# Attention queries turned two heads at a time, with the sum of squares on GpSimd

## The chip, the cores and the metric

The kernel runs on one core of one Trainium2 chip. A core has TensorE (PE; its weight loads are shown apart as PEld), VectorE (DVE), ScalarE (ACT), GpSimd (POOL) and SyncE (SP, which issues DMAs). Each engine takes its own instructions in order, and semaphores hold an instruction until what it needs is done. The metric is the device time of one execution in microseconds; less is better. Before the change it is 1444.52 us, the median of 3 runs (1444.01 to 1444.83).

## The reference, cut to what matters

One encoder layer is computed for two sequences of 512 tokens, with a model width of 1024. The input is normalized and projected to queries, keys, values, the input of a state-space branch and two gates. The state-space branch and a windowed attention branch are gated, added and projected, and a squared-ReLU MLP follows. All is float32. The part that the change touches is the norm of the queries in front of the attention:

```python
def rms_norm(x, g):
    xf = x.astype(jnp.float32)
    y = xf * lax.rsqrt(jnp.mean(xf * xf, axis=-1, keepdims=True) + EPS)
    return (y * g.astype(jnp.float32)).astype(x.dtype)

    q = rms_norm(q.reshape(bsz, seq_len, N_HEADS, HEAD_DIM), q_gain)   # 16 heads of 64
    k = rms_norm(k.reshape(bsz, seq_len, N_KV_HEADS, HEAD_DIM), k_gain)  # 4 heads of 64
    ...
    # a block of 128 queries sees the key blocks before it, at it and behind it
    s = jnp.einsum('nqkgd,njkd->nkgqj', qb, kw).astype(jnp.float32) * scale + bias
    s = jnp.where(mask[:, None, None], s, NEG_INF)
    p = jax.nn.softmax(jnp.concatenate([s, sink_col], axis=-1), axis=-1)[..., :-1]
    o = jnp.einsum('nkgqj,njkd->nqkgd', p.astype(vs.dtype), vw)
```

## The kernel before

The kernel works in stages: the load and norm of the input with the first projections, the state-space branch with the other projections between its parts, attention, the gated merge, the output projection, and the MLP. Products of float32 matrices are made in three passes from a high and a low part of each operand (a value rounded to the format fp32r, and what is left of it).

**Attention** goes over 8 steps (`steps`): 4 groups of heads `j` (one key head with its G = 4 query heads) times 2 sequences `sq`. A step has 4 units, one for each block `qb` of 128 queries; so there are 32 units. The first and the last block of a sequence see 2 key blocks, the others 3. The order of the work is written out by hand for PE, ACT, DVE and POOL; SP's DMAs follow their data. Three things run interleaved in a unit:

- `cur`, the unit itself. Per head `h`: `scores(h)` (PE, two passes, with the high and the low part of the keys), `largest(h)` (DVE, adds the bias and takes the maximum, L974), `exp(h)` (ACT, L980). Two PSUM buffers (`sps`) serve the four heads.
- `prev`, the unit before. Per key block `i`: `turn(i)` (PE, 4 transposes of the probabilities, L986), `high(i)` (ACT, L990), `low(i)` (DVE, L995), `value(i, part)` (PE, L1002). At the end `lower_part` (ACT, L1006), and in the next unit `add` (DVE, L1012).
- `new`, the tile of 128 queries of the *next* step: `project(n)` issues the next n of its 24 matmuls (L919). They fill PE between the other work. At the unit's end `square` (ACT, L925) squares the projected queries into `sq`.

In the unit after that, the tile is called `rows`. `power` sums the squares of each head (DVE, L929), adds EPS (POOL, L931) and takes the power -1/2 (POOL, L932). `norm` scales the queries (DVE, L936). `turn` makes one transpose for each of the 4 heads (PE, L941); each puts the 64 values of a head on partitions 0 to 63, in its quarter of one PSUM tile. `high` (ACT, L946) writes the high part, times the gain, to partitions 0 to 63 of the query tile `qa`, and `low` (DVE, L949) the low part to partitions 64 to 127. The key tiles hold the same 64 key values on both halves of the partitions, so that one pass of the scores multiplies the keys with high plus low part.

The order around the change, in a unit: `power` comes first; on POOL the copy of the sink into `p` (L962) stands ahead of it, and behind it stand, as far as the unit has them, pieces of the merge's operands (`y_lows`, L1066, in steps 6 and 7), the copy of the next step's keys (`key_copies`, L888, in the first unit of a step) and the low part of a weight piece (`lower`, L874 or L786). `norm` stands on DVE behind `low(0)` of `prev` and ahead of `largest(2)`. Behind `largest(3)` PE has `rows.turn`, `prev.turn(2)` (the other way round in steps 6 and 7), `key_turn` of the next keys (L901, first unit of a step), `div.turn` (second unit), four matmuls of the projection, then `rows.high`, `rows.low`, `prev.high(2)`, `prev.low(2)`, and `value(1, 0)`, `exp(3)`, four matmuls, `value(1, 1)`, four matmuls, `value(2, 0)`, `value(2, 1)`, `new.square`. From step 1 on, DVE multiplies the output of the step before with the gate at the end of the third unit (`gated`, L1047) and with the softmax's factors at the end of the fourth (`multiply`, L1051, steps 1 to 6).

Ahead of the first step a loop over t = 0 to 3 projects the first step's 4 query tiles, with `square`, `power` and `norm` at once and `turn`, `high` and `low` one tile later; the last tile is turned in the first unit. In the last step there is no next step; there `project` issues the first matmuls of the merge's product (L125).

Of the kernel before, what the change touches and what calls it, by code (L numbers as in the profile page):

```python
# [64 lines left out]
def hybrid_layer(ctx, tc, x, x_t, w_kv, rel, onehot, w_qkv, w_ug, vectors, lam, coefs, w_glu, w_out, ln2,  # L65
# [772 lines left out]
    with tc.tile_pool(name="att", bufs=2, reuse_waits="tile") as ap, tc.tile_pool(name="attc", bufs=1, reuse_waits="tile") as ac:  # L838
# [67 lines left out]
        class Tile:  # L906
# [20 lines left out]
            def power(self):  # L927
                ms = small.tile([P, G], F32, tag="ms", name="ms")
                V.reduce_sum(ms, self.sq, axis=AX.X)  # L929
                self.rq = small.tile([P, G], F32, tag="rq", name="rq")  # L930
                GP.tensor_scalar_add(ms, ms, EPS)  # L931
                GP.tensor_tensor(self.rq, ms, neg_half[:, 0:G], op=ALU.pow)  # L932
# [5 lines left out]
            def turn(self):  # L938
                self.pt = self.pt or acc()
                for h in range(G):  # L940
                    PE.transpose(self.pt[0:64, h * P:(h + 1) * P], self.qn[:, h], ident)  # L941

            def high(self):
                self.ptv = self.pt[0:64].rearrange("p (h t) -> p h t", h=G)
                self.dst = queries[self.key][:, :, self.t * P:(self.t + 1) * P]
                S.activation(self.dst[0:64], self.ptv, AF.Copy, scale=gain_q[0:64])  # L946

            def low(self):
                V.scalar_tensor_tensor(self.dst[64:128], self.ptv, gain_q[0:64], self.dst[0:64].bitcast(F32),  # L949
                                       op0=ALU.mult, op1=ALU.subtract)  # L950
# [152 lines left out]
        with tc.manual_schedule(engines={ET.PE, ET.DVE, ET.Activation, ET.Pool}):  # L1103
# [14 lines left out]
            for t in range(4):  # L1118
# [5 lines left out]
                new.power()  # L1124
# [36 lines left out]
        with tc.manual_schedule(engines={ET.PE, ET.Activation, ET.DVE, ET.Pool}):  # L1161
            for i, (j, sq) in enumerate(steps):
# [4 lines left out]
                for qb in range(NB):  # L1167
# [36 lines left out]
                    if rows and not rows.qn:  # L1204
                        rows.norm()
# [17 lines left out]
                    if n3:  # L1223
                        prev.low(1)
                        prev.value(0, 1)
                    cur.largest(3)
                    if n3 > 2 and i > 5:
                        prev.turn(2)
                    if rows:
                        rows.turn()  # L1230
                    if n3 > 2 and i < 6:
# [6 lines left out]
                    if n3 > 2 and i > 5:  # L1238
                        prev.high(2)
                        prev.low(2)  # L1240
                    if rows:
                        rows.high()
                        rows.low()
                    if n3 > 2 and i < 6:
                        prev.high(2)
                        prev.low(2)
                    if n3:
                        prev.value(1, 0)
                    cur.exp(3)
                    project(4)  # L1250
                    if n3:
# [606 lines left out]
```

## Time and profile before

| | us |
|---|---|
| median of 3 runs | 1444.52 |
| profiled execution | 1445.04 |
| its span, first to last instruction | 1443.3 |
| PE busy | 1435.6 |
| DVE busy | 1094.9 |
| ACT busy | 762.3 |
| POOL busy | 244.1 |
| attention stage, about 436 to 655: length | 219.0 |
| PE / DVE / ACT / POOL busy in it | 217.9 / 195.1 / 183.9 / 92.1 |

The clock granted to TensorE was full throughout. Matmuls overlap, so the duration of one (272 ns for a 128x128 transpose) is longer than the time for which it holds PE; that is read from the starts of instructions that follow one another. In the rows of the timeline the first number is the start in microseconds from the span's start, the second the duration of the merged run of instructions, then follow engine, line, operation, output and inputs, shape and count, and in brackets the idle time before it with what ended it. In the rows of groups the count is followed by the busy time in microseconds, the mean duration of one in nanoseconds, and the idle time ahead of them.

### The profile page before, as it was taken

To read this page: it belongs to the slowest core of one execution; us is meant where nothing else is said; L and a number is where in the kernel's file an instruction comes from. 1 tells how busy PE (TensorE), PEld (TensorE's weight loads), DVE (VectorE), ACT (ScalarE), POOL (GpSimd) and SP (SyncE) were. 2 spreads that over 40 slices of the span, in tenths; PEclk is the share of its full clock that TensorE was granted. 3 is DMA by queue.
4 is the path that set the end of the run, shared out by engine and by line. 5 is a ranking of instruction groups with operands and counts; after the bars stand their busy time and mean duration, and the time that the engine had idled before them with its cause. 6 is when DMAs were issued, how large, how long until landed. Compare 5 with 4: busy or idle time off the path is not lost.

```text
span 1443.3 us, 22044 instructions
## 1 busy us (share of the span) xinstructions
PE 1435.6 (99%) x7997; PEld 1228.0 (85%) x7997; DVE 1094.9 (76%) x1978; ACT 762.3 (53%) x1359; POOL 244.1 (17%) x396
## 2 busy tenths in 40 slices
PE   9999999999999999999999999999999999999998
PEld 8888888889999999988888888888888888888887
DVE  7999959995458999988976588777776597575644
ACT  7678861224448887894444255455454443333332
POOL 3144443004244432263100000000000000000000
PEclk9999999999999999999999999999999999999999
DMA  7356549529651533345552344444442983464341
GB/s 297 97 170 189 168 147 327 206 91 314 227 180 59 162 107 100 119 140 189 194 190 91 129 136 173 161 160 155 151 143 96 363 319 102 146 201 145 121 131 59
DMA packets 102204, 240.23 MB, mean 166 GB/s; under 512 B 12330, under 2 KB 25130, under 8 KB 102096
## 3 DMA queue, kind: packets, MB, share of 16 engines
q1 hardware_dynamic: 62304, 139.94, 29.9%
q0 software_dynamic: 16320, 48.28, 10.2%
q10 hardware_dynamic: 23472, 50.61, 9.5%
q8 instruction: 63, 1.03, 0.3%
q14 instruction: 45, 0.37, 0.1%
HBM read 169.02 MB, written 81.82 MB: 174 GB/s over the span
## 4 chain that ended last, share of the span: by engine, by line
PE 84%; DVE 8%; issue 4%; DMA 2%; ACT 1%; POOL 1%; DVEq 0%; SPq 0%; ACTq 0%; POOLq 0%
PE bank L118 14%; PE bank L120 14%; PE bank L119 14%; PE acc L187 9%; PE acc L125 6%; PE acc L919 5%; PE po L1002 2%; PE sps L970 2%; PE sps L641 2%; PE tps L986 2%; PE sps L753 2%; PE acc L120 2%; PE acc L119 2%; PE acc L118 2%; DVE t L716 2%
## 5 line engine op out<-in xcount | busy, mean ns | idle before, releaser
L187 PE MATMUL acc<-act,c_hi 128*128 128x512 f32 x768 | 243.7, 395 | 0.0
L119 PE MATMUL bank<-b_lo,a_hi 128*128 128x512 f32 (+1 forms) x449 | 174.4, 389 | 0.0
L120 PE MATMUL bank<-b_hi,a_lo 128*128 128x512 f32 (+1 forms) x449 | 174.4, 389 | 0.0
L118 PE MATMUL bank<-b_hi,a_hi 128*128 128x512 f32 (+1 forms) x449 | 174.4, 389 | 0.0
L187 PEld LDWEIGHTS acc<-act,c_hi 128*128 128x128 f32 x768 | 142.3, 188 | 27.8 <-ACT act L316 0.9
L1714 ACT CAST a_hi<-d_a 128x1024 fp32r<-128x1024 f32 x56 | 59.1, 1055 | 177.4 <-PE bank L119 173.2
L187 PE MATMUL acc<-act,c_lo 128*128 128x512 f32 x384 | 151.3, 394 | 0.0
L1715 DVE TENSOR_TENSOR a_lo<-d_a,a_hi 128x1024 fp32r<-128x1024 f32 x56 | 68.5, 1223 | 98.5 <-ACT a_hi L1714 98.5
L118 PE MATMUL bank<-act,act 128*128 128x512 f32 x368 | 143.2, 389 | 0.0
L119 PE MATMUL bank<-act,act 128*128 128x512 f32 x368 | 143.2, 389 | 0.0
L120 PE MATMUL bank<-act,act 128*128 128x512 f32 x368 | 143.2, 389 | 0.0
L919 PE MATMUL acc<-w_hi,act 128*128 128x256 f32 x512 | 114.0, 291 | 0.1
L119 PEld LDWEIGHTS bank<-b_lo,a_hi 128*128 128x128 f32 x449 | 84.3, 188 | 17.5
L120 PEld LDWEIGHTS bank<-b_hi,a_lo 128*128 128x128 f32 x449 | 84.3, 188 | 17.5
L118 PEld LDWEIGHTS bank<-b_hi,a_hi 128*128 128x128 f32 x449 | 84.3, 188 | 17.3
L919 PEld LDWEIGHTS acc<-w_hi,act 128*128 128x128 f32 x512 | 87.0, 189 | 4.0 <-PE sps L970 0.3
L187 PEld LDWEIGHTS acc<-act,c_lo 128*128 128x128 f32 x384 | 72.2, 188 | 14.7 <-DVE c_lo L178 0.8
L125 PE MATMUL acc<-act,gc_hi 128*128 128x512 f32 x256 | 81.2, 394 | 0.3 <-POOL act L1066 0.3
L118 PEld LDWEIGHTS bank<-act,act 128*128 128x128 f32 x368 | 69.1, 188 | 14.4
L120 PEld LDWEIGHTS bank<-act,act 128*128 128x128 f32 x368 | 69.1, 188 | 14.3
L119 PEld LDWEIGHTS bank<-act,act 128*128 128x128 f32 x368 | 69.1, 188 | 14.2
L980 ACT ACTIVATE p<-p,nmx 128x257 f32<-128x257 f32 (+1 forms) x128 | 72.0, 563 | 16.5 <-DVE nmx L974 15.5
(365 smaller groups left out, 3424.4 us busy)
## 6 DMA issues: line engine op xcount, KB each, us to landing
d_a<-a_scr SPq DMA_DIRECT2D x56, 512.0 KB, 3.6
raws<-in_w_up_dram SPq DMA_DIRECT2D x32, 512.0 KB, 4.0
a_scr<-t ACTq DMA_DIRECT2D x64, 256.0 KB, 3.0
k<-in_w_down_dram SPq DMA_DIRECT2D x32, 512.0 KB, 5.6
c_raw<-in_w_ug_dram SPq DMA_DIRECT2D x48, 256.0 KB, 4.1
ct_scr<-ctab POOLq DMA_DIRECT2D x16, 512.0 KB, 4.8
ctab_in<-ct_scr POOLq DMA_DIRECT2D x16, 512.0 KB, 6.4
a_scr<-a ACTq DMA_DIRECT2D x32, 256.0 KB, 2.0
```

What stands on the lines that cost most here:

```text
L118: PE.matmul(ps, a[0], b[0], start=first, stop=False)
L119: PE.matmul(ps, a[0], b[1], start=False, stop=False)
L120: PE.matmul(ps, a[1], b[0], start=False, stop=last)
L125: PE.matmul(ps, w[wi][:, k, :], rows[yi], start=k + p == 0, stop=k == KT - 1 and p == 2)
L187: PE.matmul(ps, w[wi][:, k, :], hT[s][hi][:, k, :], start=n == 0, stop=n == 3 * KT - 1)
L641: PE.matmul(ps[:, i * P:(i + 1) * P], bm[:, ri, g, :], u_sb[:, gp * SH + g, :], start=True, stop=True)
L716: V.tensor_mul(t1, h[:, i], a8r)
L753: PE.matmul(o, ctab[:, g0 % SI + g, ri, 0:T * CH], st[:, ri, g].rearrange("p s k -> p (s k)"), start=False, stop=ri == 1)
L919: PE.matmul(self.ps, hT[sq][act][:, k, col:col + P], w[:, k % 4, :], start=i == 0, stop=i == 3 * KT - 1)
L980: S.activation(p, p, AF.Exp, bias=self.nmx[:, h:h + 1], scale=-1.0, accum_out=self.sums[:, h, self.qb:self.qb + 1])
L1714: S.copy(hi, src)
L1715: V.tensor_sub(lo, src, hi.bitcast(F32))
```

## The change

The four transposes of a query tile become two. Each turns two heads (128 columns) at once, so that the even head of a pair lies on partitions 0 to 63 and the odd one on 64 to 127. The high part is written in two ACT instructions of 64 partitions x 256 elements, each to the partitions on which its heads lie, and the low part in two DVE instructions, each to the other half. For odd heads high and low part thus change places in `qa`, which the doubled keys allow.

The sum of squares is made on POOL instead of DVE: the 64 squares of each head are halved in place, 32 + 32, 16 + 16 and so on, in six additions of tensors. The four tiles ahead of the first step keep the reduction on DVE.

In a unit, `rows.norm` moves from behind `exp(1)` to just ahead of `largest(3)`. `prev.turn(2)`, `prev.high(2)` and `prev.low(2)` come first in all steps. `rows.turn` moves behind `value(1, 0)`, and `rows.high` and `rows.low` behind `exp(3)` and four more matmuls of the projection.

```diff
-            def power(self):
+            def power(self, halving=True):
                 ms = small.tile([P, G], F32, tag="ms", name="ms")
-                V.reduce_sum(ms, self.sq, axis=AX.X)
+                if halving:
+                    n = HD // 2
+                    while n > 1:
+                        GP.tensor_tensor(self.sq[:, :, 0:n], self.sq[:, :, 0:n], self.sq[:, :, n:2 * n], op=ALU.add)
+                        n //= 2
+                    GP.tensor_tensor(ms, self.sq[:, :, 0], self.sq[:, :, 1], op=ALU.add)
+                else:
+                    V.reduce_sum(ms, self.sq, axis=AX.X)
...
             def turn(self):
                 self.pt = self.pt or acc()
-                for h in range(G):
-                    PE.transpose(self.pt[0:64, h * P:(h + 1) * P], self.qn[:, h], ident)
+                for e in range(2):
+                    PE.transpose(self.pt[:, e * P:(e + 1) * P],
+                                 self.qn[:, 2 * e:2 * e + 2].rearrange("p o d -> p (o d)"), ident)
 
             def high(self):
-                self.ptv = self.pt[0:64].rearrange("p (h t) -> p h t", h=G)
-                self.dst = queries[self.key][:, :, self.t * P:(self.t + 1) * P]
-                S.activation(self.dst[0:64], self.ptv, AF.Copy, scale=gain_q[0:64])
+                ptv = self.pt[:, 0:2 * P].rearrange("p (e t) -> p e t", e=2)
+                dst = queries[self.key][:, :, self.t * P:(self.t + 1) * P].rearrange("p (e o) t -> p e o t", o=2)
+                self.parts = []
+                for o in range(2):
+                    own, other = [slice(i * 64, (i + 1) * 64) for i in (o, 1 - o)]
+                    self.parts.append((dst[other, :, o], ptv[own], gain_q[own], dst[own, :, o]))
+                    S.activation(dst[own, :, o], ptv[own], AF.Copy, scale=gain_q[own])
 
             def low(self):
-                V.scalar_tensor_tensor(self.dst[64:128], self.ptv, gain_q[0:64], self.dst[0:64].bitcast(F32),
-                                       op0=ALU.mult, op1=ALU.subtract)
+                for lo, src, gain, hi in self.parts:
+                    V.scalar_tensor_tensor(lo, src, gain, hi.bitcast(F32), op0=ALU.mult, op1=ALU.subtract)
...
-                new.power()
+                new.power(halving=False)
...
                     cur.exp(0)
                     cur.exp(1)
-                    if rows and not rows.qn:
-                        rows.norm()
...
                         prev.low(1)
                         prev.value(0, 1)
+                    if rows and not rows.qn:
+                        rows.norm()
                     cur.largest(3)
-                    if n3 > 2 and i > 5:
-                        prev.turn(2)
-                    if rows:
-                        rows.turn()
-                    if n3 > 2 and i < 6:
+                    if n3 > 2:
                         prev.turn(2)
...
                     project(4)
-                    if n3 > 2 and i > 5:
-                        prev.high(2)
-                        prev.low(2)
-                    if rows:
-                        rows.high()
-                        rows.low()
-                    if n3 > 2 and i < 6:
+                    if n3 > 2:
                         prev.high(2)
                         prev.low(2)
                     if n3:
                         prev.value(1, 0)
+                    if rows:
+                        rows.turn()
                     cur.exp(3)
                     project(4)
+                    if rows:
+                        rows.high()
+                        rows.low()
                     if n3:
                         prev.value(1, 1)
                     project(4)
```

## The prediction

> **What bounds the kernel now.** I read the page first, then busy times by stage, then the timeline of single units, engine by engine.
>
> ```profile
> span 1443.3 us, 22044 instructions
> PE 1435.6 (99%) x7997; PEld 1228.0 (85%) x7997; DVE 1094.9 (76%) x1978; ACT 762.3 (53%) x1359; POOL 244.1 (17%) x396
> ...
> 436.00:655.00 219.00, 217.89 (x1580) 201.92 (x1579) 195.13 (x504) 183.88 (x466) 92.11 (x135) 1.00 0.37 116
> 510.00:538.00 28.00, 27.96 (x210) 26.16 (x209) 25.83 (x67) 22.81 (x59) 8.73 (x15) 1.00 0.29 91
> 594.00:622.00 28.00, 27.59 (x207) 25.79 (x207) 25.23 (x66) 24.28 (x61) 13.69 (x19) 1.00 0.51 164
> ```
>
> The last three are stretches of the attention stage; behind the length stand the busy times of PE, PEld, DVE, ACT and POOL. The stage runs from about 436 to 655 us, and a step of it (four units) lasts 28 us. PE sets the pace: busy for 27.96 of 28. But DVE, at 25.83, has only 2.2 us a step to spare, and PE takes its instructions in order, so what comes late to PE costs the whole wait. POOL looks idle at 8.73; what will matter is not its load but the length of the chain that now goes through it. The profiled execution took 1445.04 us, 1.74 more than its span and 0.52 above the runs' median of 1444.52; the sum is made against 1445.04 and shifted by 0.52 at the end.
>
> **What goes from PE.**
>
> ```profile
> L941 PE MATMUL acc<-ident,qn 128*64 128x128 f32 x128 | 19.4, 274 | 0.0
> ...
> 506.00 0.60 PE L941 MATMUL acc<-ident,qn 128*64 128x128 f32 x4
> 506.44 0.60 PE L986 MATMUL tps<-ident,p 128*128 128x128 f32 x4
> ```
>
> Four query transposes hold PE from 506.00 to 506.44, 0.11 us each (the 274 ns is latency, overlapped). Of 128 the change keeps 64, now in the shape of L986's. Saved: 64 x 0.11 = **-7.0 us**, 28 of the 32 tiles in the stage and 4 just ahead of it.
>
> ```profile
> 506.87 0.61 DVE L974 CUSTOM_DVE_ANT_0 p<-sps,bias,vec 128x384 f32<-128x384 f32 x1
> 508.04 0.62 ACT L980 ACTIVATE p<-p,nmx 128x385 f32<-128x385 f32 x1
> 507.70 0.74 DVE L949 SCALAR_TENSOR_TENSOR qa<-acc,vec,qa 64x512 fp32r<-64x512 f32 x1 [0.22 <-ACT qa L946]
> 508.48 0.69 DVE L995 TENSOR_TENSOR pl<-tps,ph 128x512 fp32r<-128x512 f32 x1
> 509.08 1.22 DVE L1047 TENSOR_TENSOR ya<-ya,gate 128x1024 f32<-128x1024 f32 x1
> 509.22 0.19 PEld L1002 LDWEIGHTS po<-pl,va 128*128 128x128 f32 x1 [0.38 <-DVE pl L995]
> 509.56 0.28 PE L970 MATMUL sps<-kh,qa 128*128 128x256 f32 x1
> 510.54 0.47 DVE L974 CUSTOM_DVE_ANT_0 p<-sps,bias,vec 128x256 f32<-128x256 f32 x1
> ```
>
> In the third unit of each step the last value product waits for its low part (L995), which stands on DVE behind the queries' low part (L949). The change puts L995 first. Of PEld's 0.38 about 0.2 is lost on PE, the rest lies under the product before. Seven such units: **-1.5 us**.
>
> **What the halves and the adds cost.**
>
> ```profile
> L946 ACT ACTIVATE qa<-acc,vec 64x512 fp32r<-64x512 f32 x32 | 21.6, 673 | 0.3 <-PE acc L941 0.2
> L925 ACT ACTIVATE sq<-acc 128x256 f32<-128x256 f32 x32 | 12.3, 384 | 12.7 <-PE acc L919 12.7
> L1012 DVE TENSOR_TENSOR ya<-po,ol 64x256 f32<-64x256 f32 x64 | 26.5, 415 | 2.2 <-ACT ol L1006 1.8
> L929 DVE TENSOR_REDUCE ms<-sq 128x4 f32<-128x256 f32 x32 | 13.3, 416 | 5.9 <-ACT sq L925 5.2
> L1066 POOL TENSOR_TENSOR act<-act,act 128x512 fp32r<-128x512 f32 x16 | 20.4, 1292 | 4.5 <-ACT act L1069 4.4
> L513 POOL TENSOR_TENSOR vec<-vec,ident 128x16 f32<-128x16 f32 x2 | 0.5, 265 | 0.2
> ```
>
> ACT: one 64x512 of 0.67 becomes two of 64x256. L925, with 256 columns, takes 0.38, and no less than half of 0.67 is likely: 0.34 to 0.48 each, 0.43 taken, up to +0.3 a tile. DVE: 0.74 becomes two of 0.42 (L1012) to 0.48, +0.1 to +0.2, while the reduction's 0.42 goes. By their load both are covered by PE.
>
> POOL: six adds with 128, 64, 32, 16, 8 and 4 columns. From 0.265 at 16 and 1.292 at 512 columns I take 0.23 + 0.0021 a column: 0.50 + 0.365 + 0.30 + 0.265 + 0.25 + 0.24 = 1.92 us. Each reads what the one before wrote; the POOL rows below price that step (517.91 + 0.23 to 518.22: 0.08), six of them 0.48. So **2.40 us** stand where 0.42 stood. Bounds: six at POOL's 0.23 with the step, 1.86; 0.1 more for each, whose rows are short strips, 3.0.
>
> **Where that lands: the next keys.** First unit of a step, before:
>
> ```profile
> 516.29 0.39 ACT L925 ACTIVATE sq<-acc 128x256 f32<-128x256 f32 x1 [0.46 <-PE acc L919]
> 516.27 1.22 DVE L1051 TENSOR_TENSOR ya<-ya,fac 128x1024 f32<-128x1024 f32 x1
> 517.41 0.41 DVE L929 TENSOR_REDUCE ms<-sq 128x4 f32<-128x256 f32 x1
> 517.91 0.23 POOL L931 TENSOR_SCALAR ms<-ms 128x4 f32<-128x4 f32 x1 [5.68 <-DVE ms L929]
> 518.22 1.04 POOL L932 TENSOR_TENSOR rq<-ms,neg_half 128x4 f32<-128x4 f32 x1
> 519.22 0.62 POOL L888 COPY kd<-kn 128x512 f32<-128x512 f32 x1
> 520.50 0.62 PE L941 MATMUL acc<-ident,qn 128*64 128x128 f32 x4
> 520.95 0.60 PE L901 MATMUL tps<-ident,kd 128*128 128x128 f32 x4
> ```
>
> The copy of the next keys (kd) is queued on POOL behind the power. It is done at 519.84, and PE asks for it at 520.95: 1.1 us to spare. With the change no query turn stands ahead of the key turn, so PE asks at 520.50. The square ends at 516.68; POOL starts 0.09 later (as from 517.82 to 517.91) at 516.77; 516.77 + 2.40 + 0.23 + 0.08 + 1.04 + 0.62 = 521.14. PE waits 0.64, with the signal **0.7 us**, and all the unit's later work waits behind it. It holds in steps 1 to 6 (in step 0 the tile at hand has its norm already; step 7 has no next keys): 6 x 0.7 = **+4.2 us**; from 0.1 each (adds 1.86) to 1.3 (adds 3.0).
>
> More comes where L1051, which reads two tiles from SBUF, meets the adds. What DVE and POOL do to each other then is seen behind the stage:
>
> ```profile
> 665.30 3.41 POOL L786 TENSOR_TENSOR gc_lo<-c_raw,gc_hi 128x512 fp32r<-128x512 f32 x2 [2.57 <-ACT gc_hi L785]
> 667.59 1.67 DVE L830 TENSOR_TENSOR ga<-ga,gs 128x512 f32<-128x512 f32 x1
> 671.89 0.69 DVE L830 TENSOR_TENSOR ga<-ga,gs 128x512 f32<-128x512 f32 x1
> ```
>
> Two POOL instructions of 1.29 took 3.41 together, and L830 took 1.67 beside them against 0.69 without. They exclude each other. L1051 stands on DVE behind the queries' low halves and these behind ACT's high halves, which the change puts behind the fourth exponential; the adds begin right after the square, so both start within some tenths of each other. An add that loses waits up to 1.2. I take 0.7, for a product that starts while the first add runs and is half a microsecond ahead of the second: steps 2 to 6 (step 0 has no such product), 5 x 0.7 = **+3.5 us**, bounds 0 and 6.
>
> The Trainium skill states this as a rule ("SBUF — State Buffer", Who interferes with whom): a GpSimd instruction that reads SBUF and a VectorE one with two SBUF inputs share a port, and whichever starts first holds it to its end. The rows above agree; without the rule this term would be 0, the case of the second rival.
>
> **Where a stall goes: the product with the gate.** In the third unit L974 ends at 507.48, the fourth exponential would end at 508.1, two high halves of 0.43 at 508.9, the last low half at 509.4; then L1047, 0.3 later than its 509.08. The reduction behind it is gone, so the next unit's first maximum comes at about 510.5 as it does now. But PE, rid of transposes and stall, begins that unit at 509.1 in place of 509.56. DVE, in order, is then 0.4 later against PE through add, second maximum and low part, and the value product that needs the low part waits some 0.35: 7 x 0.35 = **+2.4 us**, from 0 to 0.5 each.
>
> **POOL in step 6.**
>
> ```profile
> 617.13 2.53 POOL L1066 TENSOR_TENSOR act<-act,act 128x512 fp32r<-128x512 f32 x2
> 619.62 1.29 POOL L786 TENSOR_TENSOR gc_lo<-c_raw,gc_hi 128x512 fp32r<-128x512 f32 x1
> 620.85 0.20 POOL L962 COPY p<-vec 128x4 f32<-128x4 f32 x1
> ```
>
> There a unit gives POOL 0.23 + 1.04 + 2.53 + 1.29 + 0.20 = 5.3 us; with the adds 7.7, against units of about 7. The queue falls behind by 0.7 in each of three units, into step 7, and the norm with it: **+2.0 us**, from 0 to 4.
>
> **The loop.** From norm to norm now runs norm 0.41, maximum 0.61, exponential 0.62, two high halves 0.86, square 0.38, signal 0.09, adds 2.40, power 1.35: 6.72 us, and a unit of PE would be (28 - 0.9 - 0.2) / 4 = 6.7. Nothing is left to spare; where the norm is late, PE waits at the query turn. I take **+1.0 us** over the stage; with the adds at their lower bound it is 0.
>
> **Sum:** -7.0 - 1.5 + 4.2 + 3.5 + 2.4 + 2.0 + 1.0 = +4.6, so 1449.6 for a profiled execution, and 1444.5 + 4.6 = 1449.1 for the median. Forecast: 1449.1, **slower**; its own range 1447 to 1454.
>
> **Rivals.**
> - Faster: the chain on POOL stays covered. If the adds take 1.86 and don't meet the products, kd is late by 0.1 (0.6), the gate costs 2.4, POOL in step 6 1.0: -8.5 + 4.0 = -4.5, 1440. It decides from adds under about 1.9 us. For it: POOL has 19 us of 28 idle. Against: L513's 0.265 for 16 columns. With DVE's lateness gone as well, -8.5, 1436.
> - No change: all as forecast, but adds and products miss each other. +3.5 and some of step 6 fall away: about +0.1, 1444.6.
> - Far slower: the loop binds. With 3.0 for the adds it lasts 7.3 against 7.0 of today's unit: 27 x 0.3 = 8, with 3.5 for the products, 0.6 more for the keys in six steps, and 2 in step 6, less 0.9 ahead of the stage: about +16, 1460. For it: the loop is already as long as the unit. Against: it needs every add 0.1 dearer than the two POOL rows price it.
> - The change doing less than it says: the 64 transposes are surely gone; at most the -1.5 fails, where L995 comes late behind the norm. That is inside the forecast's range.
>
> **Chances.** Forecast 0.5, no change 0.18, faster 0.18, far slower 0.14. A measurement of this kernel tells about 0.2%, 2.9 us, from no change. Slower by more than that: 0.14 and nearly all of 0.5, 0.62; within: 0.21; faster: 0.17. The range for 8 in 10 takes in the no-change case, the upper part of the faster one and the lower part of the far slower one: 1440.5 to 1457.
>
> **What will show it.** Right: PE or PEld waiting for the keys' copy on POOL at the key turn, about 0.7 to 1.4 us in six units; six adds on POOL of 0.23 to 0.5 us; the products L1047 and L1051, or the adds beside them, longer than alone; steps of about 28.6 in place of 28.0; no wait for the low part at the third unit's end. Wrong: steps of 27.2 with PE unbroken (faster); steps above 29.2 with PE waiting at every query turn (far slower); key turns without a wait, which would take 4 to 8 us from the sum.

## The result and the profile after

The changed kernel takes 1469.07 us (median; 1468.64 to 1469.42) against 1444.62 for the kernel before on the same chip: a ratio of 1.017, with a 95% interval of 1.0152 to 1.0187. It is slower by 24.4 us where 4.6 were forecast, and the time lies above the range. The page of the changed kernel, with the line of the whole span and the busy times:

```profile
span 1467.0 us, 22185 instructions
PE 1442.8 (98%) x7933; PEld 1221.9 (83%) x7933; DVE 1097.8 (75%) x1982; ACT 775.2 (53%) x1391; POOL 300.3 (20%) x564
```

The same five busy times for one step in the middle of the attention stage (behind the length of 31.50 us: PE, PEld, DVE, ACT, POOL):

```profile
523.60:555.10 31.50, 29.27 (x202) 25.64 (x201) 26.35 (x66) 24.64 (x63) 17.07 (x39) 1.00 0.30 88
```

Before, a step took 28.0 us with PE busy for 27.96. Now it takes 31.5. PE stands idle for 2.2 of them, and PEld, the weight loads, for 5.9 (31.50 - 25.64) where it had been 1.8 (28.00 - 26.16). DVE has hardly more to do (26.35 after 25.83). So the loss is not load. It is work that comes late, and the view of waits over the stage (engine and line that waits, what it waits for, us in total, times, longest) says on what:

```profile
ACT p L992 <- DVE nmx L986: 37.4, 58, 1.4
DVE qa L962 <- ACT qa L958: 17.4, 15, 1.6
DVE qa L962 <- PE po L1014: 13.5, 14, 1.0
PEld sps L982 <- DVE nmx L986: 13.4, 14, 1.1
PE sps L982 <- DVE nmx L986: 10.8, 14, 0.9
PEld acc L948 <- DVE qn L943: 9.3, 21, 0.9
PEld po L1014 <- DVE pl L1007: 6.5, 24, 0.3
...
PEld tps L901 <- POOL kd L888: 2.8, 6, 0.9
```

PE and its weight loads wait for DVE: for the maxima (L986), the norm (L943) and the low parts (L1007). DVE for its part waits 31 us ahead of the queries' low halves (L962). The third unit of the same step in the timeline shows both ends of this. Its own scores begin with the first row, the next unit's with the row at 546.59:

```profile
538.75 0.19 PEld L982 LDWEIGHTS sps<-kh,qa 128*128 128x128 f32 x1
539.51 0.98 DVE L962 SCALAR_TENSOR_TENSOR qa<-acc,vec,qa 64x256 fp32r<-64x256 f32 x2 [1.62 <-ACT qa L958]
539.96 1.79 POOL L932 TENSOR_TENSOR sq<-sq 128x128 f32<-128x128 f32 x5 [2.54 <-ACT sq L925]
540.52 0.62 DVE L986 CUSTOM_DVE_ANT_0 p<-sps,bias,vec 128x384 f32<-128x384 f32 x1
541.83 0.20 POOL L934 TENSOR_TENSOR ms<-sq 128x4 f32<-128x4 f32 x1
542.12 0.23 POOL L938 TENSOR_SCALAR ms<-ms 128x4 f32<-128x4 f32 x1
...
544.42 0.41 DVE L943 TENSOR_TENSOR qn<-acc,rq 128x256 f32<-128x256 f32 x1
544.75 0.61 DVE L986 CUSTOM_DVE_ANT_0 p<-sps,bias,vec 128x384 f32<-128x384 f32 x1
545.29 0.69 DVE L1007 TENSOR_TENSOR pl<-tps,ph 128x512 fp32r<-128x512 f32 x1
545.40 0.62 ACT L992 ACTIVATE p<-p,nmx 128x385 f32<-128x385 f32 x1 [0.49 <-DVE nmx L986]
546.02 0.94 ACT L958 ACTIVATE qa<-acc,vec 64x256 fp32r<-64x256 f32 x2
546.59 0.19 PEld L982 LDWEIGHTS sps<-kh,qa 128*128 128x128 f32 x1
546.99 0.98 DVE L962 SCALAR_TENSOR_TENSOR qa<-acc,vec,qa 64x256 fp32r<-64x256 f32 x2 [1.02 <-PE po L1014]
547.45 2.62 POOL L932 TENSOR_TENSOR sq<-sq 128x128 f32<-128x128 f32 x5 [2.59 <-ACT sq L925]
548.00 1.38 DVE L1059 TENSOR_TENSOR ya<-ya,gate 128x1024 f32<-128x1024 f32 x1
549.41 0.49 DVE L986 CUSTOM_DVE_ANT_0 p<-sps,bias,vec 128x256 f32<-128x256 f32 x1
549.96 0.39 PE L982 MATMUL sps<-kh,qa 128*128 128x256 f32 x1 [0.92 <-DVE nmx L986]
555.10 0.19 PEld L982 LDWEIGHTS sps<-kh,qa 128*128 128x128 f32 x1
```

DVE finishes the fourth maximum (544.75) and the third block's low part (545.29 + 0.69), then stands idle for 1.02 us until 546.99, because the high halves on ACT, behind the fourth exponential, end at 546.02 + 0.94 = 546.96. (The row names a product of PE as the releaser. By the trace that product ends at 546.98, at nearly the same time, but the low halves read nothing of it. In the unit before, where no such product ends then, ACT's pair ends at 539.47 and the low halves start at 539.51 (second row), so ACT's pair is taken as the cause here too.) The low halves, and the product with the gate behind them, hold DVE until 549.4. By then PE is 2.8 us into the next unit, and its scores of the third head wait 0.92 for the first maximum, which frees their buffer. That next unit ends at 555.10: 8.51 us. From such starts the lengths of the four units of a middle step:

| kernel | unit 1 | unit 2 | unit 3 | unit 4 | step |
|---|---|---|---|---|---|
| before | 6.66 | 6.62 | 7.62 | 7.20 | 28.1 |
| after | 8.07 | 7.09 | 7.84 | 8.51 | 31.5 |

The two units with the largest loss, 1, with +1.4, and 4, with +1.3, are those that stand behind a product of 128x1024 on DVE: with the factors (L1063) ahead of unit 1, with the gate (L1059) ahead of unit 4.

### The profile page after: what moved, and what is told of

The parts are those of the page before. It is cut to its first block, busy times and chain, and to the rows that moved or that the text cites. A ratio compares the mean times of both kernels' runs of the same rounds, so it can differ in the third digit from the quotient of the medians.

```text
span 1467.0 us, 22185 instructions
## 1 busy us (share of the span) xinstructions
PE 1442.8 (98%) x7933; PEld 1221.9 (83%) x7933; DVE 1097.8 (75%) x1982; ACT 775.2 (53%) x1391; POOL 300.3 (20%) x564
## 3 DMA queue, kind: packets, MB, share of 16 engines
q0 software_dynamic: 16320, 48.28, 10.1%
q8 instruction: 63, 1.03, 0.3%
## 4 chain that ended last, share of the span: by engine, by line
PE 77%; DVE 11%; issue 6%; ACT 3%; POOL 2%; DMA 1%; DVEq 0%; SPq 0%; ACTq 0%; POOLq 0%
PE bank L120 14%; PE bank L118 14%; PE bank L119 14%; PE acc L187 9%; PE acc L125 6%; PE acc L919 3%; PE sps L641 2%; PE sps L753 2%; PE po L1014 2%; DVE t L716 2%; DVE t L718 1%; PE acc L120 1%; PE acc L118 1%; PE acc L119 1%; DVE t L717 1%
```

## The experiments

**The three parts, alone and together.** The change has three parts: the **halves** (two heads a turn, two high and two low halves), the **sum on POOL**, and the **order** (norm behind the second keys' block, turn, high and low behind the fourth exponential, the third block's turn first). Each was taken alone, and each taken out of the changed kernel.

Halves alone: the kernel before with `turn`, `high` and `low` of the changed one.

> The kernel before with only the two-head transposes and the halves of high and low part; sum of squares on DVE, order as before. Late-halves theory (the loss comes from the queries' high and low parts standing behind the fourth exponential, so that DVE idles and the next unit's first maximum is late): the cause is absent, and of the 7.0 us of transposes most shows, 1438 to 1443 us. Two-instruction theory (the halves themselves cost the loss): slower than 1444.6 by several us, 1450 to 1465. Adds theory (the chain of adds on POOL costs it): as the first, about 1438.

The changed kernel with the sum on DVE:

```diff
-            def power(self, halving=True):
+            def power(self, halving=False):
```

> The changed kernel with the sum of squares back on DVE; two-head transposes and the new order stay. Late-halves theory: the loss stays nearly whole, 1462 to 1470 us, with DVE idle ahead of the low halves by 0.9 us or more a unit. Adds theory: the loss goes, 1438 to 1446 us. Two-instruction theory: the loss stays.

Order alone: the changed kernel with the old `turn`, `high`, `low` and the sum on DVE.

> The kernel before with only the new order (norm, turn, high and low part, third keys' block); four transposes, one high and one low instruction, sum on DVE. Late-halves theory: slower than before, 1455 to 1468 us, as one high part of 0.67 us behind the exponential delays DVE a little less than two of 0.47. Adds theory and two-instruction theory: 1443 to 1446 us, as nothing that costs is left.

Sum on POOL alone: the kernel before with the changed `power`.

> The kernel before with only the sum of squares moved to POOL (six adds), four query turns and the old order kept. Theory (VectorE's lateness sets the time, and what is given to POOL only helps where VectorE was late already): the kernel before has VectorE on time, so nothing is gained by the 0.42 us a unit; instead the norm, which still stands ahead of the third maximum, is 1.2 us later and holds VectorE there, and the next keys' copy is late: 1448 to 1458, with PE or its weight loads waiting for the norm or the third maximum. Rival (the adds are worth 8 us wherever they stand, as between the two kernels with the changed order): 1437 to 1443.

The changed kernel without the halves (old `turn`, `high`, `low`):

> The changed kernel with its order and its sum on POOL, but four query turns of one head each and one high and one low part (no halves). Theory (lateness on VectorE adds up): the order cost 15.3 with the sum on VectorE, the sum on POOL gave 8 back in that order, so 1450 to 1455, with the low part starting 0.3 to 0.5 us earlier in each unit than in the changed kernel. Rival (the halves' cost vanishes behind the late turn in the changed order, POOL's chain from square to norm sets the time): 1463 to 1469.

The changed kernel with the old order:

> The changed kernel with the old order: halves and the sum on POOL kept, the norm ahead of the third maximum and turn, high and low parts ahead of the fourth exponential again. Theory (the later norm holds VectorE ahead of the third maximum, which the new order was there to avoid, and the halves' lateness comes on top of it): 1468 to 1478, not below the changed kernel. Rival (the new order is the harm, and undoing it gives its 15 us back): 1452 to 1458.

Measured, with the ratio to the kernel before on the same chip and its interval:

| order | halves | sum | us | ratio |
|---|---|---|---|---|
| old | no | DVE | 1444.6 to 1445.1 | 1 |
| old | yes | DVE | 1456.10 | 1.0076 (1.0061 to 1.0091) |
| new | no | DVE | 1460.23 | 1.0105 (1.0088 to 1.0122) |
| new | yes | DVE | 1477.06 | 1.0221 (1.0205 to 1.0236) |
| old | no | POOL | 1464.16 | 1.0135 (1.012 to 1.015) |
| old | yes | POOL | 1472.97 | 1.0194 (1.0177 to 1.0211) |
| new | no | POOL | 1460.01 | 1.0106 (1.0089 to 1.0123) |
| new | yes | POOL | 1469.07 | 1.017 (1.0152 to 1.0187) |

Every part alone makes the kernel slower: halves 11, order 15, sum on POOL 19. They don't add up, because the new order is what makes the sum on POOL bearable: in the old order it costs 19.2, or 16.9 with the halves, in the new one 0, or with the halves it gives 8.0 back. The halves cost 9 to 17 in every company. Of the expectations, those for the halves and for the order alone held for one of their theories each, and so did the last one: undoing the order does not give its 15 us back. The theory of late halves, which held for the order, had the halves alone at 1438 to 1443 and was 13 us off there. With the sum on DVE the loss did not stay, it grew: 1477.06, 7 us above the highest expectation. The sum on POOL alone came 6 us above what either theory gave. Without the halves the changed kernel came 5 above the one theory and 3 below the other, so neither was right there: I had taken the 8 us that POOL gave with the halves to hold without them.

Why the sum on POOL costs so much alone is in that kernel's waits:

```profile
DVE qn L943 <- POOL rq L939: 25.6, 27, 1.6
PEld acc L948 <- DVE qn L943: 23.5, 27, 1.3
PE acc L948 <- DVE qn L943: 14.3, 25, 1.0
```

At its old place the norm holds DVE for POOL's chain, 25.6 us in 27 units, and the query turn on PE waits behind it. In the changed kernel the first of these waits is not among the waits of the stage at all.

**The place of the high and the low halves.** First the order's own cost, with the norm left at its old place (kernel before, the third block's turn, high and low first in all steps, the queries' turn behind `value(1, 0)`, their high and low behind the fourth exponential):

> The kernel before (four turns, sum on VectorE) with the query turn, its high and its low part behind the fourth exponential as in the change, but the norm at its old place ahead of the third maximum. With the norm moved too it was 1460.2. Theory A (the high and low part behind the fourth exponential make VectorE stand idle and the product with the gate and the next first maximum late): 1454 to 1461. Theory B (the norm's move does it): 1444 to 1449.

1454.79 us, ratio 1.0069 (1.0054 to 1.0084): ten of the fifteen come from the new places of turn, high and low part, the norm's move brings the other five. Theory A's lower end holds. Its row of the low part in the grouped lines (busy time and mean ns, then idle time ahead of it) shows DVE idle in front of it for 20 us; before, the tile's view had 5.6 us there.

```profile
L956 DVE SCALAR_TENSOR_TENSOR qa<-acc,vec,qa 64x512 fp32r<-64x512 f32 x30 | 22.3, 744 | 20.0 <-ACT qa L953 20.0
```

Then the changed kernel with both ahead of the exponential:

```diff
                     if rows:
                         rows.turn()
+                        rows.high()
+                        rows.low()
                     cur.exp(3)
                     project(4)
-                    if rows:
-                        rows.high()
-                        rows.low()
```

> The changed kernel with the high and low halves directly behind the query turn, ahead of the fourth exponential; everything else as changed. Late-halves theory: ACT makes the high halves about 0.6 us earlier and DVE idles less ahead of the low ones; a third to two thirds of the 24.4 us come back, 1452 to 1461 us. Adds theory: the norm and the keys are as late as with the change, 1464 to 1470 us.

1463.12 us, 1.0127 (1.0112 to 1.0142): 6 us back, less than the one theory's 8 and more than the other's 5. In this kernel a row of the waits that was 2.8 us in the changed one has grown, the next keys' copy:

```profile
PEld tps L901 <- POOL kd L888: 7.8, 6, 1.3
```

So the wait that the prediction had priced is larger when DVE is less late. In the changed kernel itself taking it away brings nothing:

```diff
+                    if qb == 0 and nxt:
+                        kd = key_copies(*nxt)
                     if rows and not rows.qn:
                         rows.power()
```

(the copy at its old place taken out)

> The changed kernel with one instruction moved: the copy of the next keys stands on POOL ahead of the adds. Late-halves theory: the wait for the keys is 0.5 us in each of six units and lies mostly behind DVE's lateness, so at most 3 us come back, 1465.5 to 1469 us. Late-keys theory (the predicted term): the first units of steps lose 1.4 us each to it, 8 us come back, 1460 to 1462 us.

1468.73 us, 1.017 (1.0155 to 1.0185), no change: with the keys copied first nothing comes back. The first unit of a step goes from 8.07 to 7.92 and the second from 7.09 to 7.25, so what the one gains the other loses. The changed kernel without the halves has the wait in full. Its timeline shows the copy end and PE's key turn begin:

```profile
524.67 0.61 POOL L888 COPY kd<-kn 128x512 f32<-128x512 f32 x1
525.33 0.66 PE L901 MATMUL tps<-ident,kd 128*128 128x128 f32 x4 [1.14 <-POOL kd L888]
```

**Why both low halves wait for both high halves.** In the changed kernel the first low half starts when the second high half has ended. Two layouts and two orders of writing were tried. First the heads of a half side by side in the queries' tile, in the changed kernel and in the one with the halves alone:

```diff
-    dst = queries[self.key][:, :, self.t * P:(self.t + 1) * P].rearrange("p (e o) t -> p e o t", o=2)
+    dst = queries[self.key][:, :, self.t * P:(self.t + 1) * P].rearrange("p (o e) t -> p e o t", o=2)
```

> The changed kernel with the query tile laid out so that the two heads of one half lie side by side instead of alternating with those of the other half; same instructions in the same order, same sizes. In the trace the first low half starts only when the second high half is done, though it reads only the first. Theory that this wait comes from the interleaved layout: the first low half starts about 0.47 us earlier, and 5 to 11 us come back, 1458 to 1464 us. Theory that the wait has another cause (the PSUM tile read by both): no change, 1468 to 1470 us.

> The kernel before with the two-head transposes and halves alone, as in the first experiment (1456.1 us), and the heads of one half side by side. If the wait of the first low half for both high halves makes the loss there, 4 to 7 us come back, 1449 to 1452 us; if the number and length of the DVE and ACT instructions make it, 1455 to 1457 us.

1468.53 (1.0164, 1.0148 to 1.0179) and 1455.46 (1.0072, 1.0055 to 1.0088): no change in either. Then, on top of this, each low half written directly behind its high half, and the same with a queries' tile for the even and one for the odd heads:

```diff
                     S.activation(dst[own, :, o], ptv[own], AF.Copy, scale=gain_q[own])
+                    V.scalar_tensor_tensor(dst[other, :, o], ptv[own], gain_q[own], dst[own, :, o].bitcast(F32),
+                                           op0=ALU.mult, op1=ALU.subtract)
```

> The changed kernel with the heads of a half side by side, and each low half written in the program directly behind its own high half (the order on each engine stays the same). Theory of the joint signal (the first low half starts only when both high halves are done, because only the second one signals): the first low half starts about 0.45 us earlier, behind the first high half; the low halves end 0.3 to 0.45 us earlier in 28 units, 8 to 12 us back at most: 1457 to 1463. Rival (the wait ahead of the low halves only changes its place, VectorE being late by its own load): 1465 to 1469.

> The changed kernel with the queries of the even and of the odd heads in a tile of their own each, and each low half written directly behind its high half, so that neither half waits for the other. Theory of the joint signal: the first low half starts behind the first high half, the low halves end 0.3 to 0.45 us earlier in 28 units: 1457 to 1463. Rival (VectorE is late by its own load and order, and the wait only changes its place): 1465 to 1470.

1476.26 (1.0216, 1.0201 to 1.0231) and 1476.46 (1.0217, 1.02 to 1.0234): 7 us worse, which neither theory had. ACT and DVE in the timeline of the second of these:

```profile
541.50 0.45 ACT L957 ACTIVATE qa<-acc,vec 64x256 fp32r<-64x256 f32 x1
...
541.99 0.48 DVE L958 SCALAR_TENSOR_TENSOR qa<-acc,vec,qa 64x256 fp32r<-64x256 f32 x1 [1.14 <-ACT qa L957]
...
542.50 0.47 ACT L957 ACTIVATE qa<-acc,vec 64x256 fp32r<-64x256 f32 x1 [0.55 <-DVE qa L958]
...
543.01 0.49 DVE L958 SCALAR_TENSOR_TENSOR qa<-acc,vec,qa 64x256 fp32r<-64x256 f32 x1 [0.54 <-ACT qa L957]
```

Now the first low half starts behind the first high half, but the second high half waits for the first low half, although the two write different tiles. What is left in common is what all four read, the accumulator and the gains. So ACT and DVE take it in turns in the order in which the program names them, and the four instructions last about 2 us whichever way they are written. That the accumulator is the reason is an inference: no run gave the halves accumulators of their own. The Trainium skill ("PSUM — Partial Sum Buffer", Terms) forbids two engines the same bank and quadrant at once and lets them have different quadrants of one bank. The first low half reads partitions 0 to 63 and the second high half 64 to 127, so by that rule they could run side by side. In this kernel's trace they don't. Of the 7 us, some 4 stand in two places: step 6 is 1.6 us longer, and the first unit of each of steps 1 to 5 is 0.55 longer. The square now stands 0.5 later on ACT and puts POOL's chain off, which fits the longer wait for the keys' copy; no run isolated it:

```profile
PEld tps L901 <- POOL kd L888: 5.3, 6, 1.4
```

**Is DVE the common cause?** With the halves alone, PE waits for the third block's low part, which stands on DVE behind the two low halves. The row from that kernel's waits:

```profile
PE po L1007 <- DVE pl L1000: 7.1, 12, 0.6
```

So the third block's turn, high and low part were put ahead of the queries' in all steps of that kernel:

```diff
-                    if n3 > 2 and i > 5:
+                    if n3 > 2:
                         prev.high(2)
                         prev.low(2)
                     if rows:
                         rows.high()
                         rows.low()
-                    if n3 > 2 and i < 6:
-                        prev.high(2)
-                        prev.low(2)
```

(the turns likewise)

> The first experiment (two-head transposes and halves alone, 1456.1 us) with the third keys' block of the unit before turned, split and put ahead of the queries' turn, high and low in all steps. Theory that the loss there is the third block's low part standing on DVE behind the slower query halves (PE waits 0.6 us for it at the end of two units a step): those waits go, 7 to 9 us come back, 1446 to 1450 us. Theory that DVE is simply later by the length of the halves: the wait moves to the next unit's first scores, 1453 to 1457 us.

1454.52 us, 1.0067 (1.0052 to 1.0082). The third unit is now 7.60 us, as long as before the change (with the halves alone it was 8.76), but the fourth is 7.95 instead of 7.70 and the first 7.40 instead of 6.48 (starts of units, as in the table above). The lateness is passed on, as the theory of a DVE that is simply later had it. Its timeline around the product with the gate:

```profile
540.12 0.98 DVE L955 SCALAR_TENSOR_TENSOR qa<-acc,vec,qa 64x256 fp32r<-64x256 f32 x2 [0.16 <-ACT qa L951]
540.34 0.19 PEld L975 LDWEIGHTS sps<-kh,qa 128*128 128x128 f32 x1
541.13 1.23 DVE L1052 TENSOR_TENSOR ya<-ya,gate 128x1024 f32<-128x1024 f32 x1
542.72 0.49 DVE L979 CUSTOM_DVE_ANT_0 p<-sps,bias,vec 128x256 f32<-128x256 f32 x1
543.26 0.38 PE L975 MATMUL sps<-kh,qa 128*128 128x256 f32 x1 [0.48 <-DVE nmx L979]
```

If that is the cause, the two products moved from DVE to POOL must give the time back, and give nothing in the kernel before. The same edit in three kernels:

```diff
-                V.tensor_mul(self.ya, self.ya, self.ga)
+                eng.tensor_tensor(self.ya, self.ya, self.ga, op=ALU.mult)
...
-                        late.gated()
+                        late.gated(GP)
...
-                        late.multiply()
+                        late.multiply(GP)
```

In the changed kernel:

> The changed kernel with the products with the gate and with the factors (two of 1.22 us a step on VectorE) computed on POOL. Theory (VectorE late in its order): the next unit's first maximum comes 1.2 us earlier in two of four units, 7 steps: 10 to 16 us back, 1453 to 1459. Rival (the chain from square to norm and from turn to low half sets the time): 1465 to 1470, or more where the products on POOL delay the adds.

In the kernel of the run just above, with the halves alone:

> The kernel before with the queries turned two heads at a time (sum on VectorE, old place of norm, turn, high and low part, the third block's ahead of the queries' in every step), and both products on POOL. Without the products' move this was 1454.5. Theory: VectorE loses 2.44 us a step and gains 0.6 by the halves; it is on time again and the 64 transposes that PE lost show: 1437 to 1445, faster than both kernels. Rival (the chain from turn to low half): 1451 to 1456.

In the kernel before:

> The kernel before with both products on POOL and nothing else: the control. Theory: PE is busy without a break there and VectorE is on time, so that its relief brings nothing but the third unit's wait for the low part: 1442 to 1446. If VectorE was already costing time unseen: below 1441.

1458.97 (1.0097, 1.0082 to 1.0112), 1442.87 (0.9983, 0.9974 to 0.9993) and 1443.55 (0.9989, 0.998 to 0.9998). The products give 10.1 us in the changed kernel and 11.6 with the halves alone, against 1.3 in the control. With the halves alone the fourth unit goes from 7.95 to 6.95 and the first from 7.40 to 6.40: one microsecond in each unit behind a product, none in the others. In the changed kernel it is the same pair: the fourth goes from 8.51 to 7.1 and the first from 8.07 to 7.23, while the second goes from 7.09 to 6.99 and the third stays at 7.84. A product and the beginning of the first unit behind it, in the kernel with the halves alone:

```profile
537.99 2.39 POOL L1056 TENSOR_TENSOR ya<-ya,fac 128x1024 f32<-128x1024 f32 x1
...
542.17 0.19 PEld L975 LDWEIGHTS sps<-kh,qa 128*128 128x128 f32 x1
...
543.20 0.48 DVE L979 CUSTOM_DVE_ANT_0 p<-sps,bias,vec 128x256 f32<-128x256 f32 x1
```

The first maximum comes 1.03 us into the unit; with the product on DVE it came 542.72 - 540.34 = 2.38 us into the fourth unit. And the step of the three kernels, first the halves alone, then the kernel before, then the changed kernel, each with both products on POOL, in the busy times by stage:

```profile
542.20:569.80 27.60, 27.60 (x203) 25.62 (x202) 25.09 (x68) 24.35 (x64) 13.44 (x17) 1.00 0.35 99
```

```profile
544.30:572.10 27.80, 27.78 (x210) 26.26 (x210) 23.92 (x64) 22.99 (x59) 13.45 (x17) 1.00 0.31 97
```

```profile
549.80:579.00 29.20, 28.19 (x203) 25.42 (x202) 23.60 (x64) 24.68 (x63) 20.09 (x41) 1.00 0.30 94
```

The halves with the products on POOL are the only kernel of the study with the two-head turn that isn't slower than before. But from the control it can't be told apart (1442.87 to 1443.55): PE has 64 transposes less, and a step is only 0.2 us shorter. The third line shows what is left in the changed kernel without the products on DVE: DVE has 5.6 us to spare in 29.2 and PE still waits. Rows from the waits of that kernel's stage:

```profile
PEld acc L948 <- DVE qn L943: 11.7, 21, 2.1
PEld tps L901 <- POOL kd L888: 6.2, 6, 1.4
```

Now PE waits for the norm and for the keys' copy. Against the control, the middle steps of that kernel are still 1.3 us longer, step 6 is 3.3 longer and the first three units of step 7 are 3.5 longer; what makes the loss of these two last steps was not isolated.

**A version to beat both.** The kernel before with the sum on POOL, the keys copied first and the third block first:

> The kernel before with the sum of squares on POOL, the next keys' copied on POOL ahead of the adds, and the third block's turn, high and low part ahead of the queries' in every step; four query turns, the norm at its old place. Theory as in the run with the sum on POOL alone: the keys' wait is gone, the late norm stays: 1446 to 1455. Rival (a sum on POOL costs only by the keys' copy): 1438 to 1443, faster than both kernels.

1464.09 us, 1.0134 (1.0117 to 1.0151), the same as the sum on POOL alone. The copy and the block's place don't matter there in sum: the third unit goes from 8.33 to 7.48, but the first from 7.51 to 8.16 and the fourth from 8.05 to 8.32. The norm still waits 26.3 us for POOL. That fits the late norm as the cause, but it costs more than the theory gave.

## Why the prediction was wrong

Its sign was right and its reason for the bound was right (DVE has 2 us a step to spare, PE takes its instructions in order). But of the 24 us it had found less than a fifth, and mostly in other places. That the sum came out slower at all was largely luck: the four terms that hang on the adds on POOL (+4.2, +3.5, +2.0, +1.0) make +10.7, without them the sum is -6.1, and in the changed kernel the sum on POOL costs nothing but gives 8.0 us (1477.06 to 1469.07).

**The step that failed is "Where a stall goes: the product with the gate", +2.4.** With both products off DVE 10.1 us of the 24.4 come back, so the lateness at these two places costs about four times the term, which counted one of them. It put the product 0.3 us later than before, at 509.4, in the third unit only. Counted from the unit's first scores, at 501.72 in the kernel before, that is +7.7:

```profile
501.72 0.19 PEld L970 LDWEIGHTS sps<-kh,qa 128*128 128x128 f32 x1
502.85 0.61 DVE L974 CUSTOM_DVE_ANT_0 p<-sps,bias,vec 128x384 f32<-128x384 f32 x1
```

In the changed kernel the product starts at 548.00 - 538.75 = +9.25. The 1.6 us between are made of three pieces. The fourth exponential ends at +7.3 instead of +6.4, because the fourth maximum starts at +6.0 where it had been at +5.15; the step took that maximum at its old time. Of these 0.85 us, 0.64 are there at the unit's first maximum already, at +1.77 (540.52) where it had been at +1.13 (502.85): the low halves of the queries' tile before, from 539.51 to 540.49, stand ahead of it on DVE. The other 0.2 is lost up to the fourth maximum, ahead of which the moved norm now stands. So a unit hands its lateness to the next one, and the step priced one unit that starts on time. The high halves take 0.94 instead of 0.86: +0.1 to 0.2. And the low halves start behind both high halves and take 1.01 instead of one that overlaps: +0.5. The same lateness falls on the product with the factors ahead of the first unit, which the step didn't count, and on the queries' low halves in the other units. The other 14 us are still there when the products have left DVE (1458.97 against 1444.8); the runs show waits for the norm and the keys' copy in them, but do not share them out. The product's own duration was right alone (1.22).

**"By their load both are covered by PE"** put the halves at no cost. Their durations were right or a little low: 0.455 and 0.47 each on ACT (0.94 the pair) for 0.43, 0.484 on DVE for 0.42 to 0.48. The load is not what they cost. They cost 11 alone and 9 within the change, by what they put late: once the two products had left DVE, the kernel with the halves was level with its control (1442.87 to 1443.55).

**The order** had no term of its own but the third unit's -1.5. That wait did go: in the changed kernel the weight load for that product, at 546.36, starts without one, and in the kernel with the halves alone the third block first took the third unit back to 7.60. But the order as a whole costs 15 alone, 10 by the places of turn, high and low part and 5 by the norm's. With the sum on POOL it is worth 4 (1472.97 to 1469.07; without the halves 1464.16 to 1460.01).

**-7.0 for the transposes** can't be seen. Its price per transpose was right as PE's time, but PE doesn't set the pace any more. Even where PE is without a break, with the products on POOL, a step is 0.2 shorter, not 0.9. Over such a step the time from each weight load to the next sums to 0.95 us for 8 query turns against 2.08 for 16 in the control, so PE did save it, while the same sum at the weights of the scores' low keys grew from 2.40 to 3.19. Which small wait this is was not followed further.

**The adds** were priced too high, not too low: from 539.96 to 542.12 they take 2.16 us where 2.40 were taken. The rival "far slower" came nearer in size, but from adds of 3.0, which were not there. Two of the adds by their shape, in the grouped lines (busy time, mean ns):

```profile
L932 POOL TENSOR_TENSOR sq<-sq 128x128 f32<-128x128 f32 x28 | 12.8, 456 | 74.4 <-ACT sq L925 74.4
L932 POOL TENSOR_TENSOR sq<-sq 128x16 f32<-128x16 f32 x28 | 6.2, 220 | 2.2
```

**+3.5 for adds and products that exclude each other** had the right mechanism and nearly the right size: five adds take 2.62 us beside L1059 and 1.79 alone, +0.83 for the 0.7 taken, and the product itself takes 1.38 for 1.22. Most of it falls on the third add, of 32 columns: 1.11 us beside the product and 0.26 alone, and it ends 0.11 behind the product's end. The Trainium skill's rule ("SBUF — State Buffer", Who interferes with whom) agrees with these rows. But what the adds lose delays POOL, which by the view of waits holds back neither the norm nor, to speak of, the key turn. So the clash is real and its cost in time is not seen.

**+4.2 for the next keys' copy** was real, and hidden: in the changed kernel the key turn's weight loads wait 2.8 us in six units, and copying the keys first gives nothing. It is 1.1 us on PE in the row shown of the kernel without the halves, and up to 1.3 on its weight load in the kernel with the halves ahead of the exponential. The late DVE covers it.

**+1.0 for the loop** named the right danger, nothing left to spare between norm and norm, and priced it far too low for the old order: there the norm waits 0.95 us for POOL in each of 27 units. In the new order it doesn't wait for POOL, which is as the prediction had it, but its place costs 5 (measured with the sum on DVE).

**+2.0 for POOL in step 6**: the step grew by 4.1 us, from 28.86 to 32.92, 0.7 more than a middle step (3.4). That is a third of the term and inside its range of 0 to 4; no run isolated it.

Of what should have shown it right, the adds' durations, the products' and the gone wait at the third unit's end did; the steps of 28.6 and the wait at the key turn did not. Of the signs of "far slower" both came, steps above 29.2 and loads that wait for the norm at the query turn (9.3 us in 21 units), but not its mechanism: the norm doesn't wait for POOL's loop, it stands late on DVE.

## What to carry to other kernels

Where an engine works in order and is nearly full, as DVE here with 2.2 of 28 us to spare, look for the places at which a long instruction of it stands directly ahead of something that the pacing engine needs. What delays that instruction can cost nearly its full delay there (here a product 1.6 us later, and the unit behind it 1.3 us longer), though the load hardly changes. To price a moved or split instruction, follow the whole row of instructions behind it on every engine, from the start of the unit to the next unit's first need, with all moved pieces at their new places at once, and do so for each kind of unit. To test such a cause, take other work off that engine and run the kernel before with the same edit as control.

## What was not expected of the hardware

A split into two halves was far from half: on ACT 0.67 us for 64x512 became 0.94 for the pair of 64x256, on DVE 0.745 became 0.98. POOL's two-input add did not get shorter than about 0.20 us on small shapes (0.220 at 16 columns, 0.202 at 8, 0.201 at 4), and the product of 128x1024 takes 2.39 us on POOL against 1.22 on DVE. Two instructions on ACT and two on DVE that read one accumulator ran strictly in the order written, even with outputs in separate tiles; the waits end with semaphores, so they may come from how the program is built and not from the chip. In the profile of the changed kernel with the products on POOL, PE waits 1.80 us for the norm up to 646.56, and soon after, from 647.8 to 651.2, the granted clock is 0.5. A score product of 384 columns takes 0.53 us there and 0.34 behind it. No other profile of the study shows such a stretch within the attention stage, and no run tested whether the wait brings it. The unit around it takes 7.69 us, in the changed kernel 6.55.
